# Eight of the twelve modulation chunks move from the projections of the key search to the place between the gates and the convolution branch

## The chip, the cores and the metric

The kernel runs on one core of a Trainium2 chip. The metric is the device time of one execution in microseconds. The engines are TensorE (PE), VectorE (DVE), ScalarE (ACT), GpSimd (POOL) and SyncE (SP, which issues the transfers here). Each works through its own list of instructions in a fixed order and waits where an operand or a buffer is not ready.

## The reference

One layer of a hybrid decoder on a sequence of 1024 rows and a width of 1024, in float32. The conditioning vector gives six rows of modulation; the first two are used at the very start, the other four only behind the mixer:

```python
c_act = jax.nn.silu(c)
mod = c_act @ ada_w[l] + ada_b[l]
sh1, sc1, g1, sh2, sc2, g2 = [m[:, None, :] for m in jnp.split(mod, 6, axis=-1)]
h = rmsnorm(x, mix_pre_g[l]) * (1.0 + sc1) + sh1
y = hybrid_mixer(h, ...)
x = x + g1 * rmsnorm(y, mix_post_g[l])
h = rmsnorm(x, ffn_pre_g[l]) * (1.0 + sc2) + sh2
y = conv_ffn(h, ...)
x = x + g2 * rmsnorm(y, ffn_post_g[l])
```

Inside `hybrid_mixer` one projection `z = h @ w_in` feeds four branches: A, a convolution of 31 taps with a layer norm and Silu; B, differential attention; C, stick-breaking attention; D, sparse attention, which scores all keys with a small indexer and keeps the 256 best of each query (the search). Each branch is projected and multiplied by a sigmoid gate of its own, the four are added, and the sum is projected once more.

## The kernel before

Activations lie transposed in SBUF, channels on the partitions and the 1024 rows of the sequence along the free axis, in two halves of 512. Every operand of a large matmul is split into a high and a low part (`hH`, `hL`; `whi`, `wlo`), and three products are summed. `proj` (L358) makes one tile of 128 channels: SP loads 512 KB of weights (`wraw`), ACT casts them to `whi` (L187), POOL subtracts to `wlo` (L188), PE does 24 matmuls for each half into a PSUM tile `mm` (L367), and a consumer, on ACT, evicts it. `wraw` has two buffers, `mm` two banks, and there are two more banks of a pool `ptt` for short-lived things.

The modulation comes in twelve chunks of 512 columns. `ada_chunk` (L113) loads four tiles `adaw` of 512 KB each and does eight matmuls (`adaps`, L205) on strips of 32 columns. `mod_cols` copies the result to SBUF with ACT (`adae`, L214), turns it into a column with four more matmuls (`adac`, L217), copies that with ACT (L222) and adds the bias on POOL (L223). `mod_affine` and `mod_gate` make the columns `A1`, `B1`, `A2`, `B2`, `Gm`, `Gf` of it. Chunks 0 to 3 are made at the start, because `h` needs them. Chunks 4 to 11 (`A2`, `B2`, `Gm`, `Gf`) take their `adaw` and `adae` from one ring `adq` of four slots and their two PSUM tiles from `ptt`.

In order of time the kernel makes the first projections, then the scores of the indexer (DVE, L514), then searches for the threshold of each row, in two rounds, most query tiles on DVE and some on ACT (L607 to L680; `score` at L680 writes the final mask of a tile). At the same time PE makes further projections: eight plain ones (`plain_tile`: `vc`, `vb`, `ua`), each followed by one of the chunks 4 to 11, then those of the attentions (`chi` and `czf` are the evictions of the stick-breaking attention's, L536 and L537; `sw` and `r`, L399 to L404, those with rotary positions). Behind the search come the DSA, stick-breaking and differential attentions with 22 gate projections (`gate_tile`, raw gates stored to `sg_s`) among them, then the convolution branch (L861 on): the taps have been done by DVE before, and what is left is a chain `mu` (L882), DVE (L884), square on ACT (L886), `va` (L889), root on ACT (L890), for each half, then a reciprocal on DVE (L891), the product (L893), Silu (L894) and the store to `o_s`. The merge follows: gate projections that are evicted through a sigmoid (`sgl`, L916), branch projections `brp` (L927), and products on DVE.

The order on each engine is not that of the source. A list scheduler with priorities in source order sets it when the program is built, with a model of its own for the durations; what the model sees as free early goes ahead of what was written earlier. In it the four matmul pairs of the convolution branch stand among matmuls of the first merge gates.

Of the kernel before, what the change touches and what calls it, by code (L numbers as in the profile page):

```python
# [112 lines left out]
def tile_hybrid_block(ctx, tc, x, pos, ada, pk, cst, w_in, w_br, w_out, w_up, w_dn, out):  # L113
    nc = tc.nc

    def pool(name, bufs, space=None, side=None):
        kw = {} if space is None else {"space": space}
        return tc.tile_pool(name=name, bufs=bufs, side=side, reuse_waits="tile", **kw)
# [3 lines left out]
    def dma(o, i):  # L122
        return nc.sync.dma_start(o, i)
# [7 lines left out]
    def pc(name, a=0, b=None):  # L131
        o, n = PK[name]
        return pkt[:, o + a:o + (n if b is None else b)]
# [18 lines left out]
    A2 = fix.tile([P, NK], F32, name="A2")  # L152
    B2 = fix.tile([P, NK], F32, name="B2")
    neglam = fix.tile([P, 1], F32, name="neglam")
    Gm = fix.tile([P, NK], F32, name="Gm")
    Gf = fix.tile([P, NK], F32, name="Gf")
# [69 lines left out]
    def mod_affine(m, Adst, Bdst, gname, *pools):  # L226
        md = mod_cols(m, *pools)
        c = slice(2 * (m % 4), 2 * (m % 4) + 2)
        E = V if m < 4 else G
        E.tensor_scalar(out=Adst[:, c], in0=md[:, 0:4:2], scalar1=onec, scalar2=zcol[:, 3:4], op0=OP.add, op1=OP.add)  # L230
        E.tensor_tensor(out=Adst[:, c], in0=Adst[:, c], in1=pc(gname, c.start, c.stop), op=OP.mult)
        E.tensor_copy(Bdst[:, c], md[:, 1:4:2])

    def mod_gate(m, dst, gname, *pools):
        md = mod_cols(m, *pools)
        c = slice(4 * (m % 2), 4 * (m % 2) + 4)
        (V if m < 4 else G).tensor_tensor(out=dst[:, c], in0=md, in1=pc(gname, c.start, c.stop), op=OP.mult)
# [26 lines left out]
    ptt = psx.enter_context(pool("ptt", 2, PSUM))  # L264
# [6 lines left out]
    with ExitStack() as mix:  # L271
# [11 lines left out]
        with pool("xtp", 1) as xtp, pool("adp", 8) as adp:  # L283
# [4 lines left out]
            for t in range(NT):  # L288
# [16 lines left out]
                for j0 in (0, 4):  # L305
# [3 lines left out]
                    dst = xT[:, j0:j0 + 4, t * P:(t + 1) * P]  # L309
# [181 lines left out]
        with pool("scp", 1) as scp, ExitStack() as scx:  # L491
# [52 lines left out]
            def gate_tile():  # L544
                br, c = gq.pop(0)

                def consume(hf, cs, ps):
                    o = gtp.tile([P, 512], F32, name="gt", tag="g")
                    A.copy(o, ps)
                    dma(sg_s[br * NK + c][:, cs], o)  # L550
                proj("g", br * NK + c, consume)

            adx = ExitStack()
            adq = adx.enter_context(pool("adq", 4, side="right"))
            if True:
                aq = (ptt, "t", adq, "w", adq)
                plain = [("vc", i, v_s[i], AF.Copy) for i in range(2)] + \
                    [("vb", i, v_s[2 + i], AF.Copy) for i in range(2)] + \
                    [("ua", i, ua_s[i], AF.Sigmoid if i >= 2 else AF.Copy) for i in range(4)]
                for m, (name, i, dst, func) in enumerate(plain, 4):  # L560
                    plain_tile(name, i, dst, func)
                    if m < 8:
                        mod_affine(m, A2, B2, "g2", *aq)
                    elif m < 10:
                        mod_gate(m, Gm, "p1", *aq)
                    else:
                        mod_gate(m, Gf, "p2", *aq)
            r, sw, hi, lo = small_tile("kdvd", "inv32", None, G)
            base = qkslot("kdvd", 0) * 2 * P * S
            for pcx, tl in ((0, hi), (1, lo)):  # L570
# [108 lines left out]
                    V.tensor_tensor(out=keyt(t), in0=keyt(t), in1=g_[:, :n], op=OP.add)  # L679
                    A.activation(sct(t), keyt(t), AF.Identity, scale=-NEG, bias=negc)  # L680

            adx.close()

            with pool("dp", 4) as dp, \
                    pool("da", 3) as da, pool("dot", 1) as dot, pool("ds", 8) as dsm:
# [171 lines left out]
        hi_pri.close()  # L857
        while len(gq) > 32 - NSPILL:
            gate_tile()

        hcs = []  # L861
        rst = cc.tile([P, S], F32, name="rst")
        for i in range(2):
# [6 lines left out]
            w = lambda k: pc("caw", 31 * i + k, 31 * i + k + 1)  # L870
# [32 lines left out]
        with pool("sgp", 3, side="right") as sgp:  # L903
            for bi, br in enumerate((3, 2, 1, 0)):
# [8 lines left out]
                for c in range(NK):  # L913
# [15 lines left out]
                    dst = accs[c] if bi == 0 else sg  # L929
# [131 lines left out]
    with pool("tb", 4) as tb_, pool("wsp", 1) as wsp, pool("wb", 6) as wb, pool("wr2", 2) as wr2, pool("pt", 5) as ptp:  # L1061
# [91 lines left out]
        for j in range(NF):  # L1153
# [7 lines left out]
            p1 = p1s.pop(j)  # L1161
# [151 lines left out]
```

## Time and profile before

| | us |
|---|---|
| median of 3 runs | 1996.43 |
| lowest and highest | 1993.14, 1999.46 |
| the profiled execution | 1993.31 |
| its span | 1991.5 |
| busy in the span: PE | 1809.1 (91%) |
| DVE | 1284.8 (65%) |
| ACT | 913.2 (46%) |
| POOL | 770.3 (39%) |

The mean granted clock of PE is 0.953 of full speed. Times in the trace count from the start of the span. In rows of the timeline the first number is the start and the second the duration; brackets give the idle time of the engine before the instruction and what ended it. In rows of windows each engine has its busy time in the window and, in brackets, the number of its instructions. Instructions of the same kind that follow each other are put in one row with a count, and a float32 matmul of `adaps`, `adac`, `mu` or `va` counts twice there.

### The profile page before, as it was taken

To read this page: it belongs to the slowest core of one execution; us is meant where nothing else is said; L and a number is where in the kernel's file an instruction comes from. 1 tells how busy PE (TensorE), PEld (TensorE's weight loads), DVE (VectorE), ACT (ScalarE), POOL (GpSimd) and SP (SyncE) were. 2 spreads that over 40 slices of the span, in tenths; PEclk is the share of its full clock that TensorE was granted. 3 is DMA by queue.
4 is the path that set the end of the run, shared out by engine and by line. 5 is a ranking of instruction groups with operands and counts; after the bars stand their busy time and mean duration, and the time that the engine had idled before them with its cause. 6 is when DMAs were issued, how large, how long until landed. Compare 5 with 4: busy or idle time off the path is not lost.

```text
span 1991.5 us, 23311 instructions
## 1 busy us (share of the span) xinstructions
PE 1809.1 (91%) x8528; PEld 1403.5 (70%) x8528; DVE 1284.8 (65%) x1896; ACT 913.2 (46%) x1648; POOL 770.3 (39%) x425
## 2 busy tenths in 40 slices
PE   5888968399899999999999889869999999999998
PEld 3655656277677776767787667647888888778886
DVE  6758999704799865876313485577777777743532
ACT  5555757236546564555313344444444434343321
POOL 0202136273111111101214530198888888455450
PEclk9888989699999999989999989989999999999999
DMA  8355523343623224423223454312222222265631
GB/s 316 95 136 176 191 85 96 106 113 69 200 90 99 92 84 123 98 88 106 69 74 127 143 174 138 138 43 85 85 85 85 85 75 85 95 222 166 236 127 64
DMA packets 78306, 237.18 MB, mean 119 GB/s; under 512 B 10672, under 2 KB 14896, under 8 KB 78064
## 3 DMA queue, kind: packets, MB, share of 16 engines
q1 hardware_dynamic: 78192, 235.69, 36.9%
q8 instruction: 67, 1.10, 0.2%
q14 instruction: 47, 0.39, 0.1%
HBM read 179.82 MB, written 55.84 MB: 118 GB/s over the span
## 4 chain that ended last, share of the span: by engine, by line
PE 64%; DVE 21%; ACT 4%; issue 4%; POOL 3%; DMA 3%; SPq 0%; DVEq 0%; ACTq 0%; POOLq 0%
PE ups L963 19%; PE mm L367 18%; PE dps L1191 11%; DVE junkb L607 7%; PE brp L927 3%; PE av L488 3%; PE sc L468 3%; PE yps L1011 2%; DVE hc L874 2%; PE tr L478 2%; POOL wlo L188 1%; DMA x_s<-xt 1%; PE adaps L205 1%; DVE T L620 1%; DVE th L1101 1%
## 5 line engine op out<-in xcount | busy, mean ns | idle before, releaser
L188 POOL TENSOR_TENSOR wlo<-wraw,whi 128x1024 fp32r<-128x1024 f32 x104 | 267.5, 2577 | 858.5 <-ACT whi L187 822.3
L367 PE MATMUL mm<-hH,whi 128*128 128x512 f32 x864 | 356.6, 413 | 48.3 <-ACT whi L187 30.0
L367 PE MATMUL mm<-hH,wlo 128*128 128x512 f32 x864 | 352.0, 408 | 2.7 <-POOL wlo L188 2.6
L367 PE MATMUL mm<-hL,whi 128*128 128x512 f32 x864 | 353.8, 410 | 0.3 <-DVE hL L323 0.3
L963 PE MATMUL ups<-th,wblk 128*128 128x512 f32 x1320 | 316.0, 396 | 19.5 <-DVE ub L1143 7.4
L963 PEld LDWEIGHTS ups<-th,wblk 128*128 128x128 f32 x1320 | 251.2, 191 | 77.8 <-DVE th L1101 11.5
L367 PEld LDWEIGHTS mm<-hH,whi 128*128 128x128 f32 x864 | 168.1, 195 | 94.8 <-ACT whi L187 30.4
L367 PEld LDWEIGHTS mm<-hH,wlo 128*128 128x128 f32 x864 | 167.7, 194 | 41.5 <-POOL wlo L188 3.9
L187 ACT CAST whi<-wraw 128x1024 fp32r<-128x1024 f32 x122 | 127.4, 1048 | 148.2 <-DMA wraw<-in_w_dn 57.6
L367 PEld LDWEIGHTS mm<-hL,whi 128*128 128x128 f32 x864 | 168.6, 195 | 35.6 <-issue 2.6
L942 POOL TENSOR_TENSOR wblk<-wr,wblk 128x512 fp32r<-128x512 f32 x84 | 174.2, 2084 | 8.0 <-ACT wblk L941 8.0
L1205 DVE TENSOR_TENSOR actl<-actw,acth 128x512 fp32r<-128x512 f32 x42 | 65.0, 1573 | 105.1 <-ACT acth L1204 105.1
L607 DVE TENSOR_SCALAR_CACHE_REDUCE junkb<-key,cf 128x1024 bf16<-128x1024 uint16 (+3 forms) x124 | 117.3, 946 | 4.3
L963 PE MATMUL ups<-h2h,wblk 128*128 128x512 f32 x352 | 117.2, 395 | 0.0
L942 POOL TENSOR_TENSOR wblk<-wsum,wblk 128x512 fp32r<-128x512 f32 x66 | 100.0, 1517 | 35.8 <-ACT wblk L941 35.8
L1130 DVE SCALAR_TENSOR_TENSOR ub<-ub,pkt 128x1023 f32<-128x1023 f32 x44 | 64.1, 1458 | 67.7 <-ACT ub L1129 67.7
L1191 PE MATMUL dps<-wlo,acth 128*128 128x512 f32 x336 | 104.2, 390 | 2.1 <-POOL wlo L188 2.1
L1191 PE MATMUL dps<-whi,acth 128*128 128x512 f32 x336 | 104.0, 389 | 0.0
L941 ACT CAST wblk<-wr 128x512 fp32r<-128x512 f32 x88 | 54.3, 622 | 108.2 <-PE ups L963 83.7
L1191 PE MATMUL dps<-whi,actl 128*128 128x512 f32 x336 | 103.9, 389 | 0.0
L874 DVE SCALAR_TENSOR_TENSOR hc<-hpad,pkt,hc 128x1024 f32<-128x1024 f32 x60 | 84.3, 1409 | 0.0
L1132 DVE SCALAR_TENSOR_TENSOR ub<-ub,pkt 128x1022 f32<-128x1022 f32 x44 | 83.4, 1895 | 0.8
(591 smaller groups left out, 3422.4 us busy)
## 6 DMA issues: line engine op xcount, KB each, us to landing
wraw<-in_w_in SPq DMA_DIRECT2D x54, 512.0 KB, 3.9
adaw<-in_ada SPq DMA_DIRECT2D x48, 512.0 KB, 5.9
wr<-in_w_up SPq DMA_DIRECT2D x44, 512.0 KB, 3.4
wraw<-in_w_dn SPq DMA_DIRECT2D x44, 512.0 KB, 3.4
sg_s<-gt SPq DMA_DIRECT2D x44, 256.0 KB, 2.4
sgl<-sg_s SPq DMA_DIRECT2D x22, 512.0 KB, 3.4
act_s<-ub SPq DMA_DIRECT2D x22, 512.0 KB, 2.6
actw<-act_s SPq DMA_DIRECT2D x42, 256.0 KB, 4.2
```

Source lines behind the costliest of these rows:

```text
L187: A.copy(hi, raw)
L188: (E or G).tensor_tensor(out=lo, in0=raw, in1=hi.bitcast(F32), op=OP.subtract)
L367: PE.matmul(ps, a[:, ks], b[:, k, cs], start=(n == 0), stop=(n == 3 * NK - 1))
L468: PE.matmul(ps[:, c0:c1], a, b[:, c0:c1], start=(si == 0), stop=(si == len(stacks) - 1 and not last))
L607: V.tensor_scalar(out=j[:, :n], in0=src, scalar1=scal, scalar2=None, op0=op, op1=OP.add, accum_out=dst[:, kc(t):kc(t) + 1])
L874: V.scalar_tensor_tensor(out=hc, in0=hpad[:, k:k + S], scalar=w(k), in1=hc, op0=OP.mult, op1=OP.add)
L942: E.tensor_tensor(out=b[:, 1], in0=r, in1=b[:, 0].bitcast(F32), op=OP.subtract)
L963: PE.matmul(ps, u[:, ks], v[:, k, :], start=(n == 0), stop=(n == 11))
L1130: V.scalar_tensor_tensor(out=u[:, 1:], in0=c[:, 0:S - 1], scalar=w(1), in1=u[:, 1:], op0=OP.mult, op1=OP.add)
L1132: V.scalar_tensor_tensor(out=u[:, 2:], in0=c[:, 0:S - 2], scalar=w(0), in1=u[:, 2:], op0=OP.mult, op1=OP.add)
L1191: PE.matmul(ps[:, cs], a[:, tl], b[:, cs], start=(chunk == 0 and n == 0 and i == 0), stop=(chunk == len(CH) - 1 and n == len(ops) - 1 and ...
L1205: V.tensor_tensor(out=lo, in0=raw, in1=hi.bitcast(F32), op=OP.subtract)
```

## The change

The chunks 4 to 11 are taken out of the loop over the eight plain projections, and computed in one block behind the last of the 22 gate tiles and ahead of the convolution branch. The ring `adq` keeps its four slots; it now lives only in that block. The work of a chunk is unchanged.

```diff
--- before.py
+++ after.py
@@ -550,21 +550,12 @@
                     dma(sg_s[br * NK + c][:, cs], o)
                 proj("g", br * NK + c, consume)
 
-            adx = ExitStack()
-            adq = adx.enter_context(pool("adq", 4, side="right"))
             if True:
-                aq = (ptt, "t", adq, "w", adq)
                 plain = [("vc", i, v_s[i], AF.Copy) for i in range(2)] + \
                     [("vb", i, v_s[2 + i], AF.Copy) for i in range(2)] + \
                     [("ua", i, ua_s[i], AF.Sigmoid if i >= 2 else AF.Copy) for i in range(4)]
-                for m, (name, i, dst, func) in enumerate(plain, 4):
+                for name, i, dst, func in plain:
                     plain_tile(name, i, dst, func)
-                    if m < 8:
-                        mod_affine(m, A2, B2, "g2", *aq)
-                    elif m < 10:
-                        mod_gate(m, Gm, "p1", *aq)
-                    else:
-                        mod_gate(m, Gf, "p2", *aq)
             r, sw, hi, lo = small_tile("kdvd", "inv32", None, G)
             base = qkslot("kdvd", 0) * 2 * P * S
             for pcx, tl in ((0, hi), (1, lo)):
@@ -679,7 +670,6 @@
                     V.tensor_tensor(out=keyt(t), in0=keyt(t), in1=g_[:, :n], op=OP.add)
                     A.activation(sct(t), keyt(t), AF.Identity, scale=-NEG, bias=negc)
 
-            adx.close()
 
             with pool("dp", 4) as dp, \
                     pool("da", 3) as da, pool("dot", 1) as dot, pool("ds", 8) as dsm:
@@ -857,6 +847,16 @@
         hi_pri.close()
         while len(gq) > 32 - NSPILL:
             gate_tile()
+
+        with pool("adq", 4) as adq:
+            aq = (ptt, "t", adq, "w", adq)
+            for m in range(4, 12):
+                if m < 8:
+                    mod_affine(m, A2, B2, "g2", *aq)
+                elif m < 10:
+                    mod_gate(m, Gm, "p1", *aq)
+                else:
+                    mod_gate(m, Gf, "p2", *aq)
 
         hcs = []
         rst = cc.tile([P, S], F32, name="rst")
```

The order of the instructions shifts at other places too. On ACT, at the end of the search, before:

```order
L638 ACTIVATE T_2702<-Bn 128x2
L680 ACTIVATE score<-key,zcol 128x384
L536 ACTIVATE chi<-mm 128x512
L537 ACTIVATE czf<-mm 128x512
L680 ACTIVATE score<-key,zcol 128x512
L680 ACTIVATE score<-key,zcol 128x640
L680 ACTIVATE score<-key,zcol 128x768
L680 ACTIVATE score<-key,zcol 128x896
L187 CAST whi<-wraw 128x1024 x2
L680 ACTIVATE score<-key,zcol 128x1024
L686 ACT_TABLE_LOAD
```

and after (the same place; `score` has line 671 now):

```order
L536 ACTIVATE chi<-mm 128x512
L537 ACTIVATE czf<-mm 128x512
L671 ACTIVATE score<-key,zcol 128x768
L671 ACTIVATE score<-key,zcol 128x896
L536 ACTIVATE chi<-mm 128x512
L537 ACTIVATE czf<-mm 128x512
L671 ACTIVATE score<-key,zcol 128x1024
L676 ACT_TABLE_LOAD
L187 CAST whi<-wraw 128x1024
L536 ACTIVATE chi<-mm 128x512
L537 ACTIVATE czf<-mm 128x512
L399 ACTIVATE sw<-mm 64x512
```

Before, four `score` rows in a row stand ahead of two casts `whi`, and after the last `score` come four more pairs `chi`, `czf`, before the first `sw` of L399. After, casts and pairs stand between the `score` rows (one more cast and one more pair ahead of these rows), and behind the last `score` one cast and one pair precede L399.

On PE at the convolution branch, before, with `mm` of the merge gates on both sides of each pair:

```order
L367 MATMUL mm<-hH,wlo 128x512
L367 MATMUL mm<-hH,whi 128x512
L889 MATMUL va<-hpad_4276,ones 128x512
L889 MATMUL va<-hpad_4277,ones 128x512
L882 MATMUL mu<-hc_7847,ones 128x512
L882 MATMUL mu<-hc_7883,ones 128x512
L367 MATMUL mm<-hL,whi 128x512
L367 MATMUL mm<-hH,wlo 128x512
```

and after, the last of the eight chunks and the convolution branch:

```order
L205 MATMUL adaps<-adaw,cst_c 32x512 x8
L217 MATMUL adac<-ones,adae 128x1 x4
L882 MATMUL mu<-hc_7847,ones 128x512
L882 MATMUL mu<-hc_7883,ones 128x512
L889 MATMUL va<-hpad_4040,ones 128x512
L889 MATMUL va<-hpad_4041,ones 128x512
L882 MATMUL mu<-hc_7847,ones 128x512
L882 MATMUL mu<-hc_7883,ones 128x512
L889 MATMUL va<-hpad_4040,ones 128x512
L889 MATMUL va<-hpad_4041,ones 128x512
L367 MATMUL mm<-hH,whi 128x512
```

Chunks 7 to 11 stand back to back, and `mu` and `va` without an `mm` between them. The 48 `mm` of the first merge gate and the 24 `brp` that fit beside the chain before are among chunks 4 to 6 now.

On SP, the loads of chunks 5 to 11 and what is queued behind them, after:

```order
L123 DMA adaw<-in_ada 128x1024 x4
L123 DMA wraw<-in_w_in 128x1024
L123 DMA adaw<-in_ada 128x1024 x4
L123 DMA wraw<-in_w_in 128x1024
L123 DMA adaw<-in_ada 128x1024 x20
L123 DMA o_s<-hc_7847 128x1024
L123 DMA o_s<-hc_7883 128x1024
L123 DMA wraw<-in_w_in 128x1024 x3
```

The loads of chunk 4 stand further ahead, among the stores of the gates. The two stores of the convolution branch and the weights of the merge come behind the loads of chunk 11. Between the start of the DSA attention and the last gate the order of PE's projections and attention matmuls is that of before.

## Rows read from the trace of the kernel before

**Rows 1.** the page's busy time, with its share of the span and instructions.
```profile
PE 1809.1 (91%) x8528; PEld 1403.5 (70%) x8528; DVE 1284.8 (65%) x1896; ACT 913.2 (46%) x1648; POOL 770.3 (39%) x425
```

**Rows 2.** windows, us: busy PE, PEld, DVE, ACT, POOL; PEclk, DMA, GB/s.
```profile
120.50:172.60 52.10, 43.86 (x128) 23.25 (x127) 43.65 (x52) 37.15 (x53) 8.48 (x6) 0.80 0.59 183
176.00:387.00 211.00, 149.25 (x655) 111.05 (x654) 202.16 (x427) 123.11 (x324) 71.82 (x57) 0.84 0.35 118
387.00:456.60 69.60, 65.77 (x285) 53.25 (x284) 0.03 (x1) 26.08 (x40) 47.53 (x33) 0.99 0.49 116
360.00:370.00 10.00, 0.00 (x0) 0.00 (x0) 9.72 (x12) 1.71 (x3) 1.34 (x1) 0.50 0.83 237
390.00:400.00 10.00, 10.00 (x46) 8.20 (x45) 0.00 (x0) 3.12 (x5) 4.08 (x3) 1.00 0.71 158
```

**Rows 3.** waits of PE, 340 to 392: total, times, longest.
```profile
PE mm L367 <- ACT whi L187: 30.0, 1, 30.0
```

**Rows 4.** ACT from 346 to 415: start, us, engine, line [idle before].
```profile
358.58 0.61 ACT L680 ACTIVATE score<-key,zcol 128x384 f32<-128x384 bf16 x1 [11.92 <-DVE key L679]
...
378.31 1.98 ACT L187 CAST whi<-wraw 128x1024 fp32r<-128x1024 f32 x2
387.06 1.15 ACT L680 ACTIVATE score<-key,zcol 128x1024 f32<-128x1024 bf16 x1 [6.78 <-DVE key L679]
388.23 1.28 ACT L686 ACT_TABLE_LOAD   x1
390.77 0.60 ACT L536 ACTIVATE chi<-mm 128x512 fp32r<-128x512 f32 x1 [1.26 <-PE mm L367]
...
408.03 0.58 ACT L536 ACTIVATE chi<-mm 128x512 fp32r<-128x512 f32 x1
...
412.75 0.59 ACT L399 ACTIVATE sw<-mm 64x512 f32<-64x512 f32 x1 [3.65 <-PE mm L367]
```

**Rows 5.** DVE from 380 to 458, in order of time.
```profile
384.28 2.74 DVE L679 TENSOR_TENSOR key<-key,junkb 128x1024 bf16<-128x1024 bf16 x1
456.64 1.22 DVE L710 CUSTOM_DVE_ANT_0 pd<-sc,score 128x1024 f32<-128x1024 f32 x1 [69.61 <-PE sc L468]
```

**Rows 6.** windows of the conv branch and of the merge behind it.
```profile
944.75:970.00 25.25, 24.16 (x91) 16.59 (x90) 11.49 (x7) 12.55 (x15) 6.32 (x3) 1.00 0.25 73
970.00:1100.00 130.00, 129.12 (x561) 104.54 (x560) 27.62 (x21) 28.66 (x36) 35.45 (x14) 1.00 0.27 90
```

**Rows 7.** the chain of the conv branch, on PE, DVE and ACT.
```profile
944.75 1.88 PE L882 MATMUL mu<-hc,ones 128*128 128x512 f32 x4
...
948.10 1.97 PE L889 MATMUL va<-hpad,ones 128*128 128x512 f32 x4
...
955.97 6.55 DVE L891 RECIPROCAL rst<-rst 128x1024 f32<-128x1024 f32 x1 [2.87 <-ACT rst L890]
...
965.23 2.38 ACT L894 ACTIVATE hc<-hc,pkt 128x1024 f32<-128x1024 f32 x2
...
969.57 0.50 PE L367 MATMUL mm<-hH,whi 128*128 128x512 f32 x1 [1.09 <-ACT sgl L916]
```

**Rows 8.** PE, chunk 4 among the projections ahead of the scores.
```profile
106.61 1.94 PE L205 MATMUL adaps<-adaw,cst_c 128*32 128x512 f32 x16
...
109.52 0.95 PE L217 MATMUL adac<-ones,adae 128*128 128x1 f32 x8
```

**Rows 9.** tile adaw to landing; the page's DMA issues of `wraw`.
```profile
DMA to landing us min/median/max: 3.3/5.9/7.7
...
wraw<-in_w_in SPq DMA_DIRECT2D x54, 512.0 KB, 3.9
```

**Rows 10.** PE at the first four chunks, and their window.
```profile
30.03 1.05 PE L217 MATMUL adac<-ones,adae 128*128 128x1 f32 x8 [0.73 <-ACT adae L214]
...
46.31 1.05 PE L217 MATMUL adac<-ones,adae 128*128 128x1 f32 x8 [1.68 <-ACT adae L214]
...
28.00:48.00 20.00, 14.78 (x88) 6.94 (x83) 14.36 (x26) 9.94 (x13) 0.71 (x1) 0.91 0.93 354
```

## Prediction

> **What bounds the kernel now.** The page's busy shares come first: TensorE (PE) is busy in 91% of the span [rows 1], so an edit is worth something mainly where PE is not full. The windows say where that is [rows 2]. While the search for the DSA keys runs (176 to 387 us) VectorE (DVE) is busy 202.16 of 211 us and PE only 149.25: DVE is the bound there. Behind it, from 387 to 456.6, DVE does nothing at all and PE is busy 65.77 of 69.6. The DVE rows show why: its last search instruction is at 384.28, its next at 456.64, after 69.61 us of waiting for the first attention scores [rows 5]. Those wait for projections that PE had not been able to do earlier, and the waits of PE name the stop: once, for 30.0 us, on a weight cast `whi` of ScalarE (ACT) [rows 3]. ACT's own rows show what held the cast: it stands behind the `score` activations L680, each of which waits for DVE (11.92 us the first, 6.78 the last), and comes at 378.31 [rows 4].
>
> The other place is the conv branch. From 944.75 to 969.57 a chain goes `mu`, DVE, `va`, ACT, a 6.55 us reciprocal, Silu at 965.23, and then the eviction `sgl` for which PE's next matmul waits [rows 7]. PE is nevertheless busy 24.16 of 25.25 us there, because other matmuls fill the chain; behind it PE is full, 129.12 of 130 us [rows 6]. So work that is added at this place has no slack to go into, neither there nor later.
>
> **What goes away at the search.** Eight chunks are 64 `adaps` and 32 `adac` (the trace counts each twice). Where they stood in the dense part before the scores one took 1.94 + 0.95 = 2.9 us of PE [rows 8], eight 23.2 us. Seven of the eight stood in stretches bound by DVE (chunk 5 among the scores, the others in the search), so they give PE time and no end time. Chunk 4 stood ahead of the scores, on PE's path: 2.9 us off.
>
> In the score stretch (120.5 to 172.6) 45 projection matmuls are now among the score matmuls in place of chunk 5. PE had 52.1 - 43.86 = 8.2 us free there, and 2.9 come free with the chunk: 11.1. At the full clock (46 matmuls in 10.00 us, 0.22 each [rows 2]) 45 cost 9.9 and fit; at half the clock, 0.44 each, 19.8, which is 8.7 too many. The granted clock there is 0.80 in the mean [rows 2], nearer to full, and a fuller PE speaks for more: I take 0, with 8.7 as the bad end. DVE's 211 us of search then only shift.
>
> The larger gain is the order on ACT. The changed order has a `whi` cast ahead of the first `score` row, and casts and three pairs of evictions (`chi`, `czf`) between the others; behind the last `score` only one pair remains ahead of the first eviction L399 of the differential attention's queries, where there were four, from 390.77 to 408.03. The last `score` hangs on DVE alone: 387.06, then 1.15 for itself, 1.28 for the table, 1.05 for a cast and 1.1 for the pair [rows 4]: L399 at 391.6 instead of 412.75, 21.2 us earlier. Its matmuls can be ready, if cold: 24 of 0.44 are 10.6 us, and the bank that they need is freed before the last `score`. What follows up to the first softmax is PE's and the same. Bounds: three halves fewer behind the last `score`, 72 x 0.22 = 15.8; and the whole wait, 30.0 [rows 3]. Gain: 2.9 + 21.2 = 24.1, from 2.9 - 8.7 + 15.8 = 10.0 to 32.9. It reaches the gates unchanged, because between the start of the DSA attention and the last gate the order is the same.
>
> **What comes at the new place.** The loss is what passes from the first `adaps` of chunk 4 to the last `adac` of chunk 11, since only then can `mu` and the whole chain behind it start; the chain keeps its length. Four ring slots hold the four `adaw` of a chunk and its `adae`, so a chunk's fourth load waits until the `adac` of the chunk before has read `adae`. One step of that circle: 0.73 wait on `adae` and 1.05 of `adac` [rows 10], the load, and the matmuls that stand behind it, three of the eight, 3/8 of 1.94 or 0.73 [rows 8]. The load is the unknown: `adaw` landed in 3.3 to 7.7 us, median 5.9, and weights of the same 512 KB in 3.9 [rows 9]. The long ones queued behind many; here at most three stand ahead, so I take 4.9, half way: a chunk every 7.4 us. With weights in the queue too, for chunks 5 and 6, I take 5.9: 8.4.
>
> The sum: chunk 4, whose loads are early, 4.3 (1.94, 0.73, 1.05 and a matmul or two between); chunks 5 and 6 2 x 8.4; 3 because SP, in order, holds chunk 7's loads behind a `wraw` that waits for POOL's `wlo`: 24. In this time the cover of the old chain is used up: of PE's 24.16 us the `mu` and `va` take 2 x (1.88 + 1.97) = 7.7, the other 16.5 are merge matmuls [rows 6, 7], now among chunks 4 to 6. Chunks 7 to 11 stand with nothing between: 5 x 7.4 = 37. One more us to the end of the last `adac`: 62. Then the old chain, 24.8, now with nothing beside it, and 3 us for a lower clock (`mu` and `va` alone would be 7.7 longer at half). Loss 65. Low end: the pace of the first stage, four `adac` from 30.03 to 46.31, 5.4 each [rows 10], 4.3 + 7 x 5.4 + 1 = 43; high end, with the longest load of 7.7 a chunk every 10.2: 4.3 + 7 x 10.2 + 1 + 7.7 = 84. What stands behind on SP (`o_s` stores, merge weights) waits as well, and lies inside this. Nothing gives it back, PE being full from 970 to 1100 [rows 6]; `A2` to `Gf` are not needed before that.
>
> The clock is what speaks against the place most. Rows show 0.50 at 360 to 370, inside PE's wait of 30.0 us, and 1.00 in the dense 390 to 400 [rows 2]; at 28 to 48, where chunks with their loads ran, it stayed 0.91 with PE busy 14.78 of 20 [rows 10]. The Trainium skill, "TensorE: Matmul & The Clock Gate", section "HAM oscillation — how this bites in real kernels", says that where each tile's short matmuls are followed by a longer wait for its load, the array falls back to its slow clock at every tile. By that rule all five chunks and the chain run at the lower level, which is rival (e); the trace agrees for the idle PE at the search, and not for the first stage's 0.91.
>
> **Rivals.** (a) The forecast, loads in a ring: 65 - 24 = +41.
> (b) The loads keep up as at the start, because the pace there, 354 GB/s [rows 10], needs no deeper ring: 43 - 24 = +19. Against it: there all loads were issued ahead, here the ring stops them.
> (c) No gain at the search: the matmuls among the scores cost their 8.7, or other casts stand in the way. With 0 to 10 of gain +55 to +65. For it: clocks of 0.50 around PE's idle times [rows 2]; against it the order on ACT.
> (d) The chunks cost PE's time only, loads hidden: 23.2 + 16.5 of cover = 39.7, less 24, +16. It needs early loads that the ring forbids.
> (e) Low clock throughout: `adac` and the matmuls behind the load double (1.05 + 0.73 more, for 5 chunks 9) and the chain 7.7 instead of 3: loss 79, +55.
> (f) Not slower: the 69.6 us without DVE work vanish, as all projections are done when the search ends. Then the attention starts near 391.6, gain 65, against a loss of 65 (no change) or of 40 (25 faster). It decides once the gain passes the loss. Against it: of the halves that PE does between 387 and 456 only three are ahead of the last `score` in the new order; and with the gain of 24 the chunks would have to cost 3 us each with their loads, PE's bare time.
> That the change does not do what it says is excluded: the order shows all eight chunks at the new place, and only chunk 4's loads ahead of it.
>
> **How the numbers follow.** The profiled execution is 1993.31 us (span 1991.5), 0.16% under the median 1996.43; differences are taken over to the median: (a) 2037, (b) 2015, (c) 2051 to 2061, (d) 2012, (e) 2051, (f) 1971 to 1996. Chances: (a) 0.58, (b) 0.15, (c) 0.12, (d) 0.05, (e) 0.06, (f) 0.04. About 0.3% is what a measurement tells from no change. Faster takes half of (f), 0.02; within 0.3% the other half and the edge of (d), 0.03; slower 0.95. The range leaves out (f), half of (d) and the ends of (b) and (c): 2012 to 2060.
>
> **What would show it.** Right: PE's 30 us wait near 350 to 380 gone and L399 some 20 us earlier; the first softmax 24 us earlier; `adac` rows 7 to 8 us apart behind the last gate; about 87 to 90 us from the first `adaps` there to the matmul that waits for `sgl`. Wrong: `adac` 5 to 6 us apart (b), the wait of PE on `whi` still there or the search later (c), attention directly behind the search (f).

## The result and the profile after

| | before | after |
|---|---|---|
| median, us (4 runs each) | 1997.13 | 2051.72 |
| lowest and highest | 1993.14, 1999.46 | 2048.0, 2055.59 |
| span of the profiled execution | 1991.5 | 2053.8 |
| mean granted clock | 0.953 | 0.947 |

The changed kernel takes 1.0275 of the time before, 95% interval 1.0254 to 1.0297: 54.6 us more by the medians. The profiled executions lie near opposite ends of their runs, so their spans differ by 62.3; terms read from the traces are set against that.

The busy time of PE, from the page of the changed kernel (its row of before is [rows 1]):

```profile
PE 1836.8 (89%) x8528; PEld 1409.0 (69%) x8528; DVE 1290.8 (63%) x1896; ACT 912.7 (44%) x1648; POOL 769.7 (37%) x425
```

PE's work is the same number of matmuls, and they are busy 27.7 us longer. That is a first sign that the chunks cost PE more at their new place than at the old one, though part of it can be a lower clock (0.947 against 0.953).

The end of the search on ACT, in order of time (start, duration, and idle time before; compare [rows 4]):

```profile
359.46 0.61 ACT L671 ACTIVATE score<-key,zcol 128x384 f32<-128x384 bf16 x1 [17.45 <-DVE key L670]
...
387.82 1.15 ACT L671 ACTIVATE score<-key,zcol 128x1024 f32<-128x1024 bf16 x1 [4.58 <-DVE key L670]
...
392.33 0.60 ACT L399 ACTIVATE sw<-mm 64x512 f32<-64x512 f32 x1
```

The last `score` comes at 387.82, where it came at 387.06, and the first L399 only 4.51 us behind it, where it took 25.69. L399 is 20.4 us earlier. PE's waits from 340 to 392 (total, times, longest; compare [rows 3]):

```profile
PE mm L367 <- ACT whi L187: 16.5, 1, 16.5
PE mm L367 <- ACT czf L537: 12.7, 3, 5.2
```

The one wait of 30.0 us is gone. A shorter one on the cast is left, which ends earlier, at 340.70, and three on evictions.

The new place on PE, in order of time: chunks 4 and 5, with merge matmuls of L367 between the rows shown.

```profile
931.15 1.94 PE L205 MATMUL adaps<-adaw,cst_c 128*32 128x512 f32 x16
...
934.24 1.05 PE L217 MATMUL adac<-ones,adae 128*128 128x1 f32 x8
...
938.54 1.05 PE L205 MATMUL adaps<-adaw,cst_c 128*32 128x512 f32 x2
...
940.41 1.90 PE L205 MATMUL adaps<-adaw,cst_c 128*32 128x512 f32 x6
...
943.14 1.04 PE L205 MATMUL adaps<-adaw,cst_c 128*32 128x512 f32 x2
...
945.93 1.90 PE L205 MATMUL adaps<-adaw,cst_c 128*32 128x512 f32 x6
```

Chunk 4 is whole: 16 records in 1.94 us. Chunk 5 comes in four pieces, one matmul (`x2`), three (`x6`), one, three.

Further on, one of the chunks that stand alone, from one `adac` to the next:

```profile
979.04 1.05 PE L217 MATMUL adac<-ones,adae 128*128 128x1 f32 x8 [0.72 <-ACT adae L214]
980.02 2.77 PE L205 MATMUL adaps<-adaw,cst_c 128*32 128x512 f32 x8
983.07 1.04 PE L205 MATMUL adaps<-adaw,cst_c 128*32 128x512 f32 x2 [0.28 <-DMA adaw<-in_ada]
984.35 1.90 PE L205 MATMUL adaps<-adaw,cst_c 128*32 128x512 f32 x6 [0.23 <-DMA adaw<-in_ada]
986.98 1.05 PE L217 MATMUL adac<-ones,adae 128*128 128x1 f32 x8 [0.72 <-ACT adae L214]
```

And the convolution chain, its first `mu` and the matmul at its end (compare [rows 7]):

```profile
1004.24 1.96 PE L882 MATMUL mu<-hc,ones 128*128 128x512 f32 x4
...
1029.06 0.80 PE L367 MATMUL mm<-hH,whi 128*128 128x512 f32 x1 [14.28 <-ACT sgl L916]
```

From the first `adaps` at 931.15 to the first `mu` at 1004.24 pass 73.1 us; the chain itself takes 24.8 as before, but PE ends it with 14.28 us of waiting, because no merge matmuls are left to stand beside it. Windows over the three stretches (busy PE, PEld, DVE, ACT, POOL, granted clock, DMA share, GB/s):

```profile
931.00:963.50 32.50, 32.49 (x137) 16.38 (x137) 0.00 (x0) 4.66 (x8) 6.85 (x11) 1.00 0.61 221
963.50:1004.00 40.50, 33.15 (x128) 10.81 (x128) 0.00 (x0) 3.73 (x10) 2.90 (x14) 1.00 0.66 234
1004.00:1029.00 25.00, 7.89 (x20) 3.00 (x19) 11.49 (x7) 9.52 (x13) 0.40 (x2) 0.82 0.09 37
```

PE is full up to 963.5, while three chunks pass, and then busy 33.15 of 40.50 with five chunks and the last nine merge matmuls. The clock stays at 1.00 in both, and falls to 0.82 only in the chain.

So the account at 1029 is: 13.6 us of gain (931.15 against 944.75) and 73.1 of loss, 59.5 in all. Up to the first output projection another 1.7 comes on top: PE's matmuls start 0.43 us apart behind the wait, the lower clock, for a while.

### The profile page after: what moved, and what is told of

Read it like the earlier page. It is cut to its first block, busy times and chain, and to the rows that moved or that the text cites. A ratio compares the mean times of both kernels' runs of the same rounds, so it can differ in the third digit from the quotient of the medians.

```text
span 2053.8 us, 23333 instructions
## 1 busy us (share of the span) xinstructions
PE 1836.8 (89%) x8528; PEld 1409.0 (69%) x8528; DVE 1290.8 (63%) x1896; ACT 912.7 (44%) x1648; POOL 769.7 (37%) x425
## 4 chain that ended last, share of the span: by engine, by line
PE 61%; DVE 24%; ACT 4%; DMA 4%; issue 3%; POOL 3%; SPq 0%; DVEq 0%; ACTq 0%; POOLq 0%
PE ups L963 19%; PE mm L367 16%; PE dps L1191 11%; DVE junkb L598 7%; PE av L488 3%; PE sc L468 2%; PE brp L927 2%; PE yps L1011 2%; DVE hc L874 2%; PE tr L478 2%; PE adaps L205 1%; DMA adaw<-in_ada 1%; DVE score L514 1%; DVE ge L610 1%; DMA x_s<-xt 1%
## 5 line engine op out<-in xcount | busy, mean ns | idle before, releaser
L367 PE MATMUL mm<-hH,whi 128*128 128x512 f32 x864 | 359.1, 416 | 63.1 <-ACT whi L187 16.5
L367 PE MATMUL mm<-hL,whi 128*128 128x512 f32 x864 | 355.3, 411 | 1.2 <-DVE hL L323 1.2
L367 PE MATMUL mm<-hH,wlo 128*128 128x512 f32 x864 | 353.1, 409 | 1.3 <-POOL wlo L188 1.2
L367 PEld LDWEIGHTS mm<-hH,whi 128*128 128x128 f32 x864 | 169.6, 196 | 111.4 <-ACT whi L187 17.3
L367 PEld LDWEIGHTS mm<-hL,whi 128*128 128x128 f32 x864 | 170.0, 197 | 37.9 <-issue 3.8
L367 PEld LDWEIGHTS mm<-hH,wlo 128*128 128x128 f32 x864 | 168.8, 195 | 39.6 <-issue 3.1
```

The costliest lines, as they stand in the source:

```text
L367: PE.matmul(ps, a[:, ks], b[:, k, cs], start=(n == 0), stop=(n == 3 * NK - 1))
```

## Experiments

The kernel before was run again beside each of three groups of experiments, and its median there was 1994.31 (without chunks, without loads, deep ring, first PSUM run), 1997.43 (separate `adae`, behind the branch, second PSUM run, first with `score` on DVE) and 1998.09 (the others). Differences between bare medians of two groups carry these 3 to 4 us; where it matters, the difference with each run set beside its own runs of before is given too.

### The gain alone, and where it goes

The chunks left out; the four results hold a constant:

```diff
-        with pool("adq", 4) as adq:
-            ...
+        for t_ in (A2, B2, Gm, Gf):
+            G.memset(t_, 0.5)
```

> Left out: the chunks 4 to 11; A2, B2, Gm and Gf hold the constant 0.5. Everything else is the changed kernel. It gives the gain alone. In the changed kernel the first instruction of the new place starts 13.6 us earlier than in the kernel before (931.15 against 944.75). Theory: this gain reaches the end, because PE is full behind it: 1997.1 - 13.6 = 1983.5, and the convolution branch takes its 24.8 us again. Rival 1, what was forecast: 24.1 of gain, 1973. Rival 2: the gain is lost behind the gates, 1997.

Measured: 1979.43 us, ratio 0.992 (0.9901 to 0.9939). First `mu` and the matmul behind `sgl`, on PE:

```profile
929.25 1.88 PE L875 MATMUL mu<-hc,ones 128*128 128x512 f32 x4
...
954.06 0.50 PE L367 MATMUL mm<-hH,whi 128*128 128x512 f32 x1 [1.07 <-ACT sgl L909]
```

The branch starts 15.5 us earlier than before and takes its 24.8 again. The gain is 14.9 us beside its own runs of the kernel before (1994.31), and what is there at the branch reaches the end. What the changed kernel loses at the new place is 2051.7 - 1979.4 = 72.3 us by bare medians, 54.6 + 14.9 = 69.5 with each beside its own runs of before.

### What the loss is made of

**Without loads.** Chunks 5 to 11 use the weight tiles of chunk 4 (and `adae` has a pool of its own, not shown):

```diff
+                if len(kept) == 5:
+                    pts.append(kept[1 + g])
+                    continue
                 pt = wr.tile([P, D], F32, name="adaw", tag="w")
                 dma(pt, ada[m, g])
```

> Changed computation: chunks 5 to 11 take the four weight tiles that chunk 4 loaded, so only chunk 4 loads, and adae has a pool of its own; matmuls, copies and places of all eight chunks stay. Theory (the loads set the pace of 8.2 us a chunk): what is left is PE's own time, 8 x 2.9 = 23 us, partly among the merge matmuls, so the loss falls from 73 to about 23 to 30, and the time is 1983.5 + 23 to 30 = 2007 to 2014. Rival (the circle adaps, adae, adac itself is slow): little changes, 2045 or more.

Measured: 2010.87 us, 31.4 over the kernel without chunks. The last chunk and the chain behind it, on PE:

```profile
954.33 1.94 PE L212 MATMUL adaps<-adaw,cst_c 128*32 128x512 f32 x16
...
958.03 1.96 PE L890 MATMUL mu<-hc,ones 128*128 128x512 f32 x4
...
982.86 0.79 PE L374 MATMUL mm<-hH,whi 128*128 128x512 f32 x1 [8.33 <-ACT sgl L924]
```

A chunk takes 3.78 us from `adaps` to `adaps`, with `adac` and the merge matmuls between, and all eight 30.5 us. The loads are thus 40.9 of the 72.3 us (38.0 of the 69.5), directly or through what they do to the order: without them all eight chunks stand whole, each `adaps` group 1.94 us.

**A deep ring.**

```diff
-        with pool("adq", 4) as adq:
+        with pool("adq", 12) as adq:
```

> Only the ring adq is deeper: 12 slots for 4. Theory (a chunk's fourth load waits for the adac before it): the loads now go ahead by two chunks and run at the bandwidth, 7 chunks of 2.1 MB at 354 GB/s are 41.5 us for 73, and merge matmuls stand beside the convolution chain again: 2052 - 25 to 32 = 2020 to 2027. Rival 1 (transfers themselves take 8 us a chunk): 2052. Rival 2 (loads would be wholly hidden): 2010.

Measured: 2026.15 us. Two chunks in the middle, on PE:

```profile
953.01 3.46 PE L205 MATMUL adaps<-adaw,cst_c 128*32 128x512 f32 x16
957.14 1.05 PE L217 MATMUL adac<-ones,adae 128*128 128x1 f32 x8 [0.68 <-ACT adae L214]
958.13 3.46 PE L205 MATMUL adaps<-adaw,cst_c 128*32 128x512 f32 x16
```

A chunk every 5.12 us, all eight back to back, 44.4 us from the first `adaps` to `mu`; the price over the kernel without chunks is 46.7. This is the pace that the first stage showed (5.4, [rows 10]). The four slots are worth 25.6 us (22.8 with each beside its own runs of before).

**The circle through `adae`.**

```diff
-        with pool("adq", 4) as adq:
-            aq = (ptt, "t", adq, "w", adq)
+        with pool("adq", 4) as adq, pool("ade", 2) as ade:
+            aq = (ptt, "t", ade, "e", adq)
```

> The changed kernel with adae in a pool of its own (two buffers); the ring of four slots holds only the adaw. A chunk's fourth load then no longer waits for the adac before it. Theory (the circle through adae is what lengthens a chunk from 5.1 us, measured with the deep ring, to 8.2): a chunk takes 5.1 to 6.5 and the time is 2026 to 2038. Rival (four slots are too few for the transfers by themselves, each load waits for the matmuls on its slot): 8 us a chunk, 2046 to 2052.

Measured: 2050.4 us, no difference that can be told. One chunk of the last four, on PE:

```profile
984.54 2.64 PE L205 MATMUL adaps<-adaw,cst_c 128*32 128x512 f32 x10
987.58 1.90 PE L205 MATMUL adaps<-adaw,cst_c 128*32 128x512 f32 x6 [0.40 <-DMA adaw<-in_ada]
990.21 1.05 PE L217 MATMUL adac<-ones,adae 128*128 128x1 f32 x8 [0.73 <-ACT adae L214]
```

Where the chunks stand alone the pace did fall, from 8.2 to 6.5 us a chunk (`adac` to `adac`), so the circle is there. But the order changed too: one more chunk now stands in pieces among the merge matmuls, and the first four chunks take 42.5 us where the first three took 32.4. The time tells nothing between the theories; the pace alone does.

**Behind the convolution branch.** The same block with the same ring, some lines further down in the source:

```diff
             gate_tile()
-        with pool("adq", 4) as adq:
-            aq = (ptt, "t", adq, "w", adq)
...
             dma(o_s[i], hcs[i])
+        with pool("adq", 4) as adq:
+            aq = (ptt, "t", adq, "w", adq)
...
```

> The block of eight chunks, with its ring of four slots, stands behind the convolution branch in the source and not ahead of it; nothing else is changed from the changed kernel. In the order of PE the chunks are then among the matmuls of the first merge gates, 3 to 12 of them between each two steps, and the convolution chain comes first. Theory (the loss of 72 us is the wait for loads with nothing beside it; the work itself costs PE 2.9 a chunk): over the kernel without chunks (1979.4) 23 us for the matmuls and up to 12 for waits, 2003 to 2015. Rival (the price is that of eight chunks through a ring of four slots, wherever they stand): 2045 to 2052.

Measured: 2027.69 us, between theory and rival, 48.3 over the kernel without chunks (45.1 with each beside its own runs of before). PE does not wait there at all (0.7 us in 920 to 1060), and still pays twice what was expected. Its rows show for what:

```profile
976.76 0.40 PE L367 MATMUL mm<-hL,whi 128*128 128x512 f32 x1
977.08 1.04 PE L205 MATMUL adaps<-adaw,cst_c 128*32 128x512 f32 x2
978.06 0.50 PE L367 MATMUL mm<-hH,wlo 128*128 128x512 f32 x1
...
978.86 0.39 PE L367 MATMUL mm<-hH,wlo 128*128 128x512 f32 x1
979.18 1.90 PE L205 MATMUL adaps<-adaw,cst_c 128*32 128x512 f32 x6
981.02 0.51 PE L367 MATMUL mm<-hH,whi 128*128 128x512 f32 x1
```

Matmuls of L367 start 0.23 apart. A piece of one `adaps` lies between 976.99, where the next one would have started, and 978.06: 1.07 us. A piece of three lies between 979.09 and 981.02: 1.93 us, as much as all eight take when they stand together. A chunk in four pieces costs 6.0 and with its `adac` 6.95, not 2.9. Two chunks of the eight are not cut up like that (the first is whole, the last partly): 2.9 + 6 x 6.95 + 4.1 = 48.7. In the trace, matched matmul by matmul against that of the kernel without chunks, 50.9 us are lost between the branch and the end of the last chunk.

The eight write four strips of 32 columns, and what the rows show is that matmuls on different strips run beside each other if they follow each other, and that other matmuls between them end that. The Trainium skill says the first of these in "TensorE: Matmul & The Clock Gate", section "Part 3: Packing small matmuls — row/col tiling": small tiles of the array work at the same time. What it costs to break such a group up stands in the rows here.

**The same, in one piece.** The matmul whose tile is loaded last is issued first, so that nothing can come between:

```diff
-        for g0 in (0, 2):
-            ...
+        for gs in ((0, 1), (2, 3)) if m < 4 else ((3, 2, 1, 0),):
+            ...
             for r in range(2):
-                for g in (g0, g0 + 1):
+                for g in gs:
```

> As behind (ring of four slots, block behind the convolution branch, among the merge matmuls), but a chunk's eight adaps are issued with those of the last load first, so that in PE's order they stand together and not in pieces of 1, 3, 1 and 3 among other matmuls. In the trace of behind a piece of one costs 1.07 us and a piece of three 1.93, 6.0 a chunk with 0.95 of adac behind, where eight together take 1.94; 2.9 + 6 x 6.95 + 4.1 is 48.7, and behind is 48.3 slower than the kernel without chunks. Theory (the pieces are the price): 1979.4 + 8 x 2.9 = 2003, up to 2008 with a few waits. Rival (waits for loads that the order hides): 2020 to 2028.

Measured: 2017.57 us. A chunk on PE, the last one, and the only long wait of PE between 920 and 1060 (total, times, longest):

```profile
946.73 1.92 PE L204 MATMUL adaps<-adaw,cst_c 128*32 128x512 f32 x16
...
949.86 0.95 PE L216 MATMUL adac<-ones,adae 128*128 128x1 f32 x8
...
1014.65 3.64 PE L204 MATMUL adaps<-adaw,cst_c 128*32 128x512 f32 x16 [6.37 <-DMA adaw<-in_ada]
```

```profile
PE adaps L204 <- DMA adaw<-in_ada: 9.6, 3, 6.4
```

Each of the first six chunks costs about 1.92 and 0.95 again, though others stand between it and the next. The last two, which the order has back to back, wait for their loads and take 20.8 us (1000.00 to 1020.78). Over the kernel without chunks it is 38.1 us by bare medians, 34.4 with each beside its own runs of before. Matched in the trace as above, 39.2 are lost between the branch, which this execution reached 4.1 us earlier than the one without chunks (925.12 against 929.25), and the end of the last chunk; 6 x 2.9 and 20.8 account for 38.2. So the pieces were a large part of the price of the run before, waits for loads took part of it back, and the theory missed the two chunks at the end.

### Why the search did not get shorter

The search starts 6.2 us earlier than before (first counts at 166.94 against 173.10) and ends 0.8 later. Two rows of DVE in the changed kernel, and one of POOL at the same time:

```profile
190.44 0.61 DVE L598 TENSOR_SCALAR_CACHE_REDUCE junkb<-key,cf 128x384 bf16<-128x384 int16 x1
...
191.10 1.83 DVE L610 TENSOR_TENSOR ge<-cnt,kreq 128x4 f32<-128x4 f32 x1
```

```profile
190.49 2.42 POOL L188 TENSOR_TENSOR wlo<-wraw,whi 128x1024 fp32r<-128x1024 f32 x1 [8.37 <-ACT whi L187]
```

DVE's `ge` works on four columns. It starts while POOL's `wlo` runs, and ends, 1.83 us later, when `wlo` ends (192.91). The instructions of this tile in the search (min/median/max in ns) show how unequal they are:

```profile
L610 DVE TENSOR_TENSOR ge<-cnt,kreq x31: 161/164/1995, 181.0 to 354.4; 128x4 f32<-128x4 f32 x31
L611 DVE SCALAR_TENSOR_TENSOR T<-ge,T x31: 161/162/1206, 182.2 to 354.6; 128x4 f32<-128x4 f32 x31
```

These three small instructions (`ge`, `T`, `cf`) took 28.9 us of the search before and 30.9 now, 2.0 of the 6.9 by which it grew. The rest stands in larger ones, `eqb` and `key` of the masks, 28.0 us before and 33.7 now (one pair of small `kq` gave 0.9 back). One of them, before and after:

```profile
264.37 0.35 DVE L656 TENSOR_SCALAR eqb<-key,T 128x512 bf16<-128x512 int16 x1
```

```profile
266.19 2.75 DVE L647 TENSOR_SCALAR eqb<-key,T 128x512 bf16<-128x512 int16 x1
```

After, POOL's `sw` and `wlo` follow each other from 264.42 to 268.80, and `eqb` ends at 268.94. For these the cause is read from such rows alone; the runs below change the small ones only.

There are such rows before as well (the longest `T` of before takes 3.73 us, over three instructions of POOL); which of DVE's instructions meet one of POOL's, and for how long, is set by when PE asks for weights. **First experiment**: two of the small operands, the counts and the flags `ge`, in PSUM.

```diff
+                psm = ptt.tile([P, 512], F32, name="psm", tag="t")
+                kreqp, gep = psm[:, 0:NB], psm[:, 16:16 + NB]
...
-    V.tensor_tensor(out=ge[:, v], in0=cnt[:, v], in1=kreq[:, v], op=OP.is_ge)
+    V.tensor_tensor(out=gep[:, v], in0=cnt[:, v], in1=kreqp[:, v], op=OP.is_ge)
```

> The changed kernel, with two small operands of DVE's search (the required counts, and the flags ge) in PSUM instead of SBUF; nothing else. In the trace of the changed kernel eleven of these instructions on four columns, 0.16 us elsewhere, take 0.5 to 2.0 us and end together with a wlo subtraction or rotary product of POOL; the search is 6.6 us longer in DVE time than before. Theory (DVE's instruction with two SBUF operands waits for POOL's): they take their 0.16 again (up to 0.3 with PSUM), the search ends about 5 us earlier and the time is 2047. Rival (they wait for something else, the counts of ACT's half or a semaphore): same durations, 2052; with slower PSUM reads, 2 to 4 us more.

Measured: 2057.16 us, 5 slower (8 with each beside its own runs of before). The two instructions that now have one operand in PSUM, and the third, `cf`, that has not:

```profile
L613 DVE TENSOR_TENSOR psm<-cnt,psm x31: 166/167/168, 223.9 to 388.7; 128x4 f32<-128x4 f32 x31
L614 DVE SCALAR_TENSOR_TENSOR T<-psm,T x31: 157/161/163, 224.1 to 388.9; 128x4 f32<-128x4 f32 x31
...
L610 DVE TENSOR_SCALAR cf<-T x31: 164/182/1316, 166.7 to 384.5; 128x4 f32<-128x4 f32 x31
```

None of the 62 is held any more; the 31 of `cf`, from SBUF to SBUF, are held instead, up to 1.3 us. This much bears the theory out. The time says nothing about it, since DVE stood 44.3 us before it could first write the new tile (`issue` in the trace, in a pool of two banks that the projections use).

**Second and third experiment**: threshold and counts in PSUM, so that all three have an operand there, first in the same pool, then in that of the scores, which is free in the search:

```diff
-    psm = ptt.tile([P, 512], F32, name="psm", tag="t")
+    psm = pss.tile([P, S], F32, name="psm", tag="s")
...
+    kreqp, T = psm[:, 0:NB], psm[:, 16:16 + NB]
```

> The changed kernel with the required counts and the threshold T of DVE's search in PSUM from the start, so that each of the three small instructions of a search step has at most one operand in SBUF, and the step's addition none; the flags ge are in SBUF again. Theory (DVE's small instructions are held by POOL's while both operands, or the input and the output, are in SBUF): the three of all 31 steps, 30.9 us together in the changed kernel, take 31 x 3 x 0.17 = 16, the search ends up to 14 us earlier and the time falls to 2038 to 2046. Rival 1: they are held all the same, 2052. Rival 2: the search ends earlier, but the projections behind it set the start of the attention, so less than 5 us of it arrive, 2047 to 2052.

Measured: 2047.64 us. DVE stood 46.7 us for the same reason, and yet the first softmax came 18.7 us earlier than in the changed kernel (422.9 against 441.59): the projections went on meanwhile and were done when the search ended. But the second softmax came at 444.55, behind the 442.73 of the changed kernel, so that early start is worth little. The run tells the small instructions' time, 15.1 us for 93, and nothing of the search's.

> As lock2, with the PSUM tile in the pool of the scores, which is free during the search, since in lock2 DVE stood 46.7 us before it could first write the tile. Theory: without that wait the search is 14 us shorter than in the changed kernel, and with it the last score activation and all behind it come 10 to 15 us earlier: 2037 to 2042. Rival 1 (what the search gives, the projections behind it take back): 2047 to 2052. Rival 2 (another wait for the tile): slower.

Measured: 2037.82 us, 13.9 under the changed kernel (14.9 with each beside its own runs of before), and DVE no longer stands before its first write. The three instructions in that run:

```profile
L610 DVE TENSOR_SCALAR cf<-psm x31: 160/161/164, 174.8 to 334.0; 128x4 f32<-128x4 f32 x31
L613 DVE TENSOR_TENSOR ge<-cnt,psm x31: 157/157/160, 179.0 to 338.2; 128x4 f32<-128x4 f32 x31
L614 DVE SCALAR_TENSOR_TENSOR psm<-ge,psm x31: 166/167/168, 179.2 to 338.4; 128x4 f32<-128x4 f32 x31
```

The longest takes 168 ns, where it was 1995. The last `score` comes at 371.76 instead of 387.82, L399 at 376.28 instead of 392.33, and nearly all of it arrives. This confirms the theory in both its halves: the holds of these instructions cost DVE 14 to 16 us in the search, and the search sets the end.

The Trainium skill tells of this in "SBUF — State Buffer", section "Who interferes with whom": VectorE and GpSimd share a pair of ports, and VectorE instructions with two inputs in SBUF, or in the forms that use both ports, wait until a GpSimd instruction that has the pair is over. The runs agree in each form: two inputs in SBUF held up to 2.0 us, one in PSUM never, the copying form with SBUF on both sides held, from PSUM never.

### The order on ACT, and a version that beats both

In the kernel before, with the chunks at their old place, the same PSUM operands, and then also the six `score` on DVE:

```diff
-    A.activation(sct(t), keyt(t), AF.Identity, scale=-NEG, bias=negc)
+    V.tensor_scalar(out=sct(t), in0=keyt(t), scalar1=-NEG, scalar2=NEG, op0=OP.mult, op1=OP.add)
```

> The kernel before, chunks at their old place, with the threshold and the counts in PSUM as in lock2, and the six score activations at the end of the search on DVE instead of ACT. ACT's weight casts and evictions then stand behind nothing that DVE has still to make. Theory (PE's 30.0 us wait came from that order on ACT): that wait goes, PE does projections in it, DVE's search is 14 us shorter by the held instructions and 5 longer by the six; the first softmax comes 25 to 35 us earlier and the time is 1960 to 1970. Rival 1 (POOL's wlo or the loads set the projections' pace): 5 to 15 us, 1980 to 1990. Rival 2: nothing, 1994.

Measured: 2014.12 us, slower than before. This had the tile in the pool of two banks, and DVE stood three times in the search, together 82 us, 24.0 of them at the first write of the tile. It says nothing on the order on ACT.

> The kernel before, chunks at their old place, with the search's threshold and counts in PSUM as in lock3. Theory: 31 steps x 3 instructions take 16 us for 28.9, so the search ends 13 us earlier, the score activations and the weight casts behind them too, and PE's wait of 30.0 shrinks by as much: 1997 - 13 = 1984. Rival (other matmuls or POOL's wlo become the limit behind the search): 1990 to 1997.

Measured: 1984.74 us, 0.9935 of the time before (0.9919 to 0.9952). PE's wait on the cast (total, times, longest):

```profile
PE mm L367 <- ACT whi L187: 24.5, 1, 24.5
```

The forecast of the time holds, 13.4 us, and L399 comes at 400.01 for 412.75. The wait did not shrink by as much, from 30.0 to 24.5: PE's end of it moved with the search, and its start too.

> As fast4, and the six score activations at the end of the search made by DVE, so that ACT's casts and evictions stand behind nothing that waits for DVE. Theory: PE's wait on the cast goes, projections move into it, at the price of 5 us more on DVE: 10 to 20 us under fast4, 1965 to 1975. Rival (the projections are held by POOL or by ACT's own half of the search): as fast4 or up to 5 slower.

Measured: **1971.22 us, 0.9869 of the time before (0.9854 to 0.9884)**, with the chunks at their old place. The same wait:

```profile
PE mm L367 <- ACT whi L187: 11.0, 1, 11.0
```

With nothing of DVE's ahead of them the casts come earlier, and the first softmax at 434.1 for 459.12. Of the 11.0 that are left ACT itself waits 8.49 for a load of `wraw`. This step alone gave 13.5 us over the run before it, nearly what the change gained in passing (14.9), and no chunk moved for it. So the larger part of that gain, the 21.2 us behind the last `score`, came from the order on ACT. The 6.2 us ahead of the search, where chunks 4 and 5 had stood, are another matter.

## Why the prediction was right, and where its steps were not

The forecast was 2037, the range 2012 to 2060, and 2051.72 lies in it. Mechanism and sign hold; two terms were too small on the bad side (by 8 us together) and one too large on the good one (by 10), so that 41 us became 59.5 in the trace at the branch and 54.6 by the medians. The number alone does not speak for (a): 2051 to 2061 was the figure of (c), 2051 that of (e). The rows do, as below. That the errors did not carry the time out of the range is owed to the range's width, not to the sum.

**What bounded the kernel.** Right: the 30.0 us of [rows 3] came from the order on ACT, as the run with `score` on DVE shows (11.0 left). In the changed kernel the sign that was named, this wait gone, came true for the one long wait only; 16.5 and 12.7 us of shorter ones on ACT are left.

**Gain.** The tail was sized exactly: L399 followed the last `score` by 25.69 us and now by 4.51, 21.2 less as forecast. Chunk 4's 2.9 us also (first score product at 118.82 for 121.71). The score stretch, taken as 0 with 8.7 as the bad end, gave 3.3. The step that failed is "DVE's 211 us of search then only shift": from its first count to its last instruction it grew from 213.9 to 220.8, by DVE instructions that end with POOL's, small ones and those of the mask. With it 20.4 of 24.1 us were there at L399. Of these 6.8 are gone at the new place (13.6 left): the first softmax is 17.5 us earlier, the first gate 17.3, the last 13.7. Matched matmul by matmul, the lead of the changed kernel falls by 1.6 between 474 and 500, where PE waits 0.79 for a load of `qds` that it had not waited for and the granted clock over 487 to 491 is 0.55 to 0.59 (1.00 over 492 to 506 before), and by 1.9 at 731.64, where PE waits 1.75 for a load of `vt`, again new; the rest goes in small steps. Why these loads come later for PE, and what the 2.9 between L399 and the first softmax are, no run takes apart; this part stays open. The words "It reaches the gates unchanged" were wrong by that: the same order met other states of clock and loads.

**Loss.** Forecast 65, measured 73.1 in the trace and 69.5 to 72.3 by the medians. By terms:

| term | forecast | measured |
|---|---|---|
| chunks 4 to 6 | 24 | 32.4 |
| chunks 7 to 11 | 37 + 1 | 40.7 |
| lower clock in the chain | 3 | 0 (1.7 behind it) |

The first two were short by the same thing: the price of matmuls that stand in pieces. Chunks 4 to 6 are PE's own time, and not the loads by which the forecast had sized 5 and 6, since PE was full there: 2.9 + 2 x 6.95, and 63 of the 72 merge matmuls at 0.23, 14.5, make 31.3 of the 32.4. The other nine, 2.1, lie in the 40.7. In the circle of chunks 7 to 11 the "three of the eight" behind the last load, put at 0.73, take 1.90. With 0.72 and 1.05 a load of 4.5 is left of the 8.2 (the trace gives 3.2 to 5.1 to landing there, median 4.2), close to the 4.9 chosen, and that was the number that had been called the unknown. The 1.94 and 2.9 us from [rows 8], taken for every chunk, were the price of one that happened to stand whole.

**The clock.** Rival (e) fell: 1.00 through both stretches with chunks. The rule that the Trainium skill gives in "TensorE: Matmul & The Clock Gate", section "HAM oscillation — how this bites in real kernels", had no effect between the chunks here: PE was busy 33.15 of 40.50 us, its waits for one load at most 0.78 in the rows. Where it did wait, in the chain, the clock fell to 0.82, but the chain's length is that of DVE and ACT. In the run with whole chunks behind the branch PE waited 2.78 and then 6.37 us for the loads of the last two, and the granted clock was 0.50, the lower of its two levels, from 1014 to 1023; there the trace agrees with that rule. Shorter waits do not always spare it either: in the changed kernel it fell to 0.55 to 0.59 over 487 to 491, behind waits of 0.79 and 1.37 us for `qds`.

**The other rivals.** (b) is what the ring of twelve slots gives: 46.7, not 43, with 5.12 a chunk. (d), 39.7 for PE's time alone, is nearly the run without loads (31.4), where the cover of the chain was partly kept. (c) was too dark in its reason, since the score stretch cost nothing and the order on ACT did give; its gain of 0 to 10 is nearer to the 13.6 than the forecast's 24.1. (f) did not occur in the changed kernel; the second PSUM run (lock2) shows that the first softmax can follow the last `score` at once, when DVE is late enough for the projections to be done.

## What to carry to other kernels

Before moving small matmuls into a full stretch of PE, look whether they stand whole where their price was read: cut up by the order they cost more than twice as much here (6.95 us for 2.9). Work with its own loads belongs where something can stand beside it, and its ring must hold the next piece's loads before the last result is read. When a move changes the order of an engine that casts for another, read first what that engine waits for there; the gain may be had without the move.

## What the runs showed of the hardware that was not expected

- A DVE instruction on four columns, 0.16 us, takes up to 2.0 us while POOL works on SBUF (once 3.7 in the kernel before), and 0.17 at most with an operand in PSUM. Over 31 search steps this made 29 to 31 us of 15.
- Eight matmuls on four strips of 32 columns take 1.94 us together, and 6.0 in pieces of 1, 3, 1 and 3 among others.
- The granted clock stayed 1.00 over 40 us in which PE waited for loads again and again, up to 0.78 us each; behind waits of 0.79 and 1.37 us elsewhere in the same run it fell to 0.55 to 0.59.
